# One layer of a hybrid delta-rule and latent-attention encoder: the prompt's latent query projection placed between the two input projections, narrower products in the block inverse, a shared half of PSUM

## Chip, cores and metric

One Trainium2 chip, one core. The metric is device time of one execution in microseconds, the median of several runs.

## What is computed

One encoder layer for two sequences that share weights: a prompt of 1024 tokens (`p`) and a sample of 512 (`s`). All is float32 at the interface.

```
h    = rmsnorm(x);  proj = h @ w_in                    # 2048 -> 5984 columns
qkv  = silu(conv5(qkv))                                # delta-rule heads, 8 of 128
o_a  = gated delta rule forward + backward             # chunks, one inverse per chunk
q    = rmsnorm(c_q) @ w_uq ; kv = rmsnorm(c_kv) @ w_ukv
o_b  = dense softmax attention over all positions      # 8 heads, rope on 64 columns
y    = concat(o_a*silu(z_a), o_b*silu(z_b)) @ w_out
out  = x + rmsnorm(y)
```

## The kernel before

A dense product is three TensorE products: operands are split into a rounded `hi` (float32r) and a rest `lo`, and hi·hi, lo·hi and hi·lo are summed in one PSUM bank (`piece`, L199 to L208, loads a weight piece of 128x512 on SP's queue; `split`, L192 to L197, makes `whi` on ACT and `wlo` on POOL; `ktile`, L218 to L229, issues the products `mm` of L224, L225 and L228). The small products of the delta rule are plain float32, which the profile records as two passes each.

The stages, in order of the program (`run`, from L1221):

1. **Input projection of the prompt** (`in_proj("p", ...)`). For each 128 columns of `w_in` (a strip, 47 of them) 16 k-tiles are summed into two banks. The first two strips run while x arrives, normalised later by `rbh`, which `bcast_cols` makes out of row sums (`xcols`, L275; `bcp`, L190).
2. **Input projection of the sample** (`in_proj("s", ...)`), one bank to a strip, merged with the **delta rule** (`gdn_streams`). The delta rule runs 12 jobs, 8 of one prompt head and 4 of two sample heads, in three streams: `gdn_front` (the masked decays `bc`, L668 and L669, the products `kk`, and a 31-step elimination on VectorE), `gdn_back` (the block inverse: `Dp`, `Fp`, then three rounds of `Tp` at L791 with 128, 64 and 32 moving columns), and `gdn_scan` (per chunk `pk`, `py`, `pu`, each of which waits for VectorE or ScalarE to take up the product before it).
3. **`mla_prep`** for the latent queries: three blocks of 512 tokens (two of the prompt, one of the sample), 12 strips `pq` each, 12 matmuls to a strip (L558 to L560), merged with the delta rule that is still running.
4. **Attention** of the prompt, then of the sample (`kp`, `vp`, `s`, `pt`, `po`), merged with the rest of the delta rule; once the delta rule has ended, with the first half of the **output projection** (`first()`, L1272).
5. The rest of the output projection alone.

In the merged stages the order of TensorE's instructions is written out by `merge` (L136): every stream yields a time at which it wants to go on, `self.t` counts modelled TensorE time (`cost`, L116: 0.42 ns for a column and pass), and the first stream in the list whose time has come is asked next. A stream of the delta rule yields `self.t + self.lat` or `self.t + self.tlat` after each step, so that other streams fill the wait. TensorE executes this order strictly; the other engines' orders come from the scheduler. Outside `merge` the scheduler orders TensorE too.

PSUM in stages 1 and 2 is one pool for each `in_proj`: 6 banks `mm` and 2 `tk` for the prompt, 3 and 1 for the sample beside 4 of the delta rule. Stage 2's pools are opened when those of stage 1 are closed.

Of the kernel before, what the change touches and what calls it, by code (L numbers as in the profile page):

```python
# [17 lines left out]
P = 128  # L18
# [39 lines left out]
class Kern:  # L58
    def __init__(self, ctx, tc, a):
# [21 lines left out]
        self.cols = {}  # L81
        self.t, self.streams, self.leaving, self.busy = 0.0, None, False, [0.0, 0.0]

    def constants(self):
        nc, c, load = self.nc, self.const, self.load
        self.ident = self.kept.tile([P, P], F32, tag="ident", name="ident")
        nc.sync.dma_start(self.ident, self.a["ident"])
# [10 lines left out]
        self.identb = c.tile([P, P], BF16, tag="identb", name="identb")  # L98
        nc.vector.tensor_copy(self.identb, self.ident)
# [81 lines left out]
    def bcast_cols(self, cols, n, ps, out, scale=1.0, tag="tk"):  # L181

        nc = self.nc
        for c0 in range(0, n, 4):
            m = min(4, n - c0)
            pb = ps.tile([P, BLK], F32, tag=tag, name="bcp", bufs=self.tkb)
# [45 lines left out]
    def in_proj(self, q, T, pools, lo_eng, ns, pace):  # L232
        nc, a = self.nc, self.a
        cp, hps, hp, ev, psmm = pools
        psb = psmm
# [7 lines left out]
        newps = lambda: [psmm.tile([P, BLK], F32, tag="mm", name=f"mm{b}") for b in range(nb)]  # L243
# [29 lines left out]
        cols = psb.tile([P, nt], F32, tag="tk", name="xcols", bufs=self.tkb)  # L273
# [7 lines left out]
        yield self.t + BC  # L281
        self.bcast_cols(r, nt, psb, rbh, scale=0.5)

        later = []
        for f in order:
# [9 lines left out]
            if f < 32 or ZB0 <= f < LAST:  # L295
# [20 lines left out]
                if f < 8:  # L316
                    later.append(self.sums(q, f, T, t, acc, cp, ev, psmm))
                if 8 <= f < 24:
                    later.append(self.to_tokens(q, f, T, t, acc, cp, psmm))
            else:  # L320
# [5 lines left out]
                if f < ZB0:  # L326
# [5 lines left out]
                    if f in (CKV0 - 1, ZB0 - 1):  # L332
                        later.append(self.csums(q, f, T, sq, psmm))
                if f == LAST:
                    later.append(self.gates(q, T, acc, ev, psb))

    def sums(self, q, f, T, t, sq, ev, xp, psmm):
# [8 lines left out]
        for b in range(T // BLK):  # L346
            ps = psmm.tile([P, BLK], F32, tag="tk", name="sumps", bufs=self.tkb)
# [14 lines left out]
        ps = psmm.tile([P, H * C], F32, tag="tk", name="qcols", bufs=self.tkb)  # L362
# [23 lines left out]
    def csums(self, q, f, T, sq, psmm):  # L386
# [3 lines left out]
        ps = psmm.tile([P, C], F32, tag="tk", name="csumps", bufs=self.tkb)  # L390
# [7 lines left out]
        yield self.t + 9  # L398
        ps = psmm.tile([P, P], F32, tag="tk", name="crow", bufs=self.tkb)
# [5 lines left out]
    def to_tokens(self, q, f, T, t, sq, ev, psmm):  # L405
# [6 lines left out]
        for c0 in range(0, C, 4):  # L412
            ps = psmm.tile([P, 4, P], F32, tag="tk", name="tokps", bufs=self.tkb)
# [17 lines left out]
    def gates(self, q, T, acc, ev, psb):  # L431
# [4 lines left out]
        for c0 in range(0, C, 8):  # L436
            ps = psb.tile([P, 8, 64], F32, tag="tk", name="abps", bufs=self.tkb)
# [28 lines left out]
        pg = psb.tile([P, 2, C, 16], F32, tag="tk", name="gps", bufs=self.tkb)  # L466
# [4 lines left out]
        yield self.t + 3  # L471
# [13 lines left out]
        for c0 in range(0, C, 4):  # L485
            ps = psb.tile([32, BLK], F32, tag="tk", name="gtps", bufs=self.tkb)
# [13 lines left out]
    def mla_prep(self, blocks, rp, hp, pp, qp, psb):  # L500
# [32 lines left out]
        for b, (q, t0) in enumerate(blocks):  # L533
# [18 lines left out]
            for n, f in enumerate((8, 0, 1, 9, 2, 3, 10, 4, 5, 11, 6, 7)):  # L552
# [3 lines left out]
                ps = psb.tile([P, BLK], F32, tag="pm", name="pq", bufs=PMB)  # L556
# [190 lines left out]
    def gdn_back(self, turn, q, T, heads, env, KQ, UA):  # L747
# [3 lines left out]
        for items in (((0, 0), (1, 4)), ((0, 4), (1, 0))):  # L751
# [469 lines left out]
    def run(self, stop=None):  # L1221
        tc, nc = self.tc, self.nc
        self.tkb, self.wb, self.rb = 2, 4, 4
# [6 lines left out]
        def in_pools(es, q, mm):  # L1230
# [8 lines left out]
            return cp, hps, hp, ev, pool(es, "ps" + q, mm, space=PSUM)  # L1239
# [7 lines left out]
        self.tkb, self.wb, self.rb = 1, 3, 2  # L1247
        with ExitStack() as es:
            env = self.gdn_open(gd, right)
            gdn = self.gdn_streams(jobs, env)  # L1250
            self.merge(self.in_proj("s", TS, in_pools(es, "s", 3), nc.gpsimd, 2, 0.6), gdn)
# [141 lines left out]
```

## Time and profile before

| | |
|---|---|
| median of 3 runs | 3361.96 us (3359.56 to 3369.88) |
| the profiled execution's own time | 3363.58 us |
| its span | 3361.7 us |
| mean granted TensorE clock | 0.983 |
| TensorE (PE) busy | 3212.2 us, 96% of the span |
| VectorE, ScalarE, GpSimd busy | 1735.1, 1283.6, 1158.5 us |
| DMA | 381.66 MB, mean 114 GB/s |

The busy time of TensorE is a union of overlapping records (a matmul is listed with 0.39 us where the next starts 0.23 us later), so the price of a matmul is read from the distance of two starts in the timeline. The granted clock is 1 at 2.4 GHz and 0.5 at 1.2 GHz, and a window's clock is a mean of the two.

### The profile page before, as it was taken

Reading aid. Unit: us, or ns where it says so; the run is one execution under the profiler, and the core shown is the slowest. Engines: PE = TensorE matmul, PEld = TensorE weight load, DVE = VectorE, ACT = ScalarE, POOL = GpSimd, SP = SyncE. Lnnn points to the kernel's source line nnn. Section 1 sums busy time; section 2 is a strip of 40 time slices with the busy share of each in tenths; the row PEclk is TensorE's granted clock in tenths of the full one; section 3 lists DMA queues with packets and bytes.
Section 4 is the critical chain, followed back from the end, with each engine's and each line's share of the span. In section 5 each row is a group of like instructions: output and inputs, shape, how many; then the busy total and the mean of one; then the engine's idle time right before and its main releaser. Section 6 shows DMA issues by size and latency. Waiting matters only on the chain.

```text
span 3361.7 us, 46959 instructions
## 1 busy us (share of the span) xinstructions
PE 3212.2 (96%) x16554; PEld 2688.5 (80%) x16554; DVE 1735.1 (52%) x4000; ACT 1283.6 (38%) x2956; POOL 1158.5 (34%) x1026
## 2 busy tenths in 40 slices
PE   8999999999999899999999989899999989999998
PEld 6888888888887688788788777688898878787876
DVE  7234333443412656774775577688787655331212
ACT  4222222222212334444345334365656555432231
POOL 6322222222223532332332334222222444464452
PEclk9999999999999899999999999899999999999999
DMA  4222222222223534334433466522222242564454
GB/s 159 83 73 79 72 78 75 78 72 79 84 75 105 159 100 126 116 107 129 131 111 120 135 211 206 155 82 70 89 76 64 99 135 86 155 186 135 143 168 135
DMA packets 271404, 381.66 MB, mean 114 GB/s; under 512 B 75632, under 2 KB 126824, under 8 KB 269632
## 3 DMA queue, kind: packets, MB, share of 16 engines
q1 hardware_dynamic: 271168, 378.66, 37.0%
q8 instruction: 130, 2.13, 0.3%
q14 instruction: 106, 0.87, 0.1%
HBM read 286.73 MB, written 88.29 MB: 112 GB/s over the span
## 4 chain that ended last, share of the span: by engine, by line
PE 65%; DVE 15%; DMA 10%; issue 3%; ACT 3%; POOL 2%; SPq 1%; POOLq 0%; DVEq 0%; ACTq 0%
PE mm L224 13%; PE mm L228 12%; PE mm L225 12%; DMA wraw<-w_out 3%; PE py L1152 3%; PE py L1151 3%; PE py L1153 3%; DVE tm L737 3%; DVE XT L739 2%; PE Tp L791 2%; POOL wlo L199 2%; PE pt L1074 2%; DMA wraw<-w_in 1%; DVE UA L686 1%; DVE acc L306 1%
## 5 line engine op out<-in xcount | busy, mean ns | idle before, releaser
L199 POOL TENSOR_TENSOR wlo<-wraw,whi 128x512 fp32r<-128x512 f32 x620 | 832.3, 1346 | 1610.4 <-ACT whi L196 1522.3
L224 PE MATMUL mm<-hi,whi 128*128 128x512 f32 x2256 | 910.6, 405 | 16.9 <-ACT whi L196 11.7
L225 PE MATMUL mm<-lo,whi 128*128 128x512 f32 x2256 | 884.7, 393 | 8.1 <-DVE lo L255 8.1
L196 ACT ACTIVATE whi<-wraw 128x512 fp32r<-128x512 f32 x620 | 389.0, 631 | 1181.5 <-PE mm L225 693.4
L228 PE MATMUL mm<-hi,wlo 128*128 128x512 f32 x2256 | 767.5, 394 | 1.6 <-POOL wlo L199 1.5
L224 PEld LDWEIGHTS mm<-hi,whi 128*128 128x128 f32 x2256 | 429.3, 190 | 101.1 <-ACT whi L196 13.7
L228 PEld LDWEIGHTS mm<-hi,wlo 128*128 128x128 f32 x2256 | 427.7, 190 | 97.1 <-POOL wlo L199 5.0
L225 PEld LDWEIGHTS mm<-lo,whi 128*128 128x128 f32 x2256 | 429.4, 190 | 92.7 <-DVE lo L255 10.0
L1151 PE MATMUL py<-whi,mhi 128*128 128x512 f32 x768 | 304.1, 396 | 9.9 <-DVE y L1166 5.6
L1152 PE MATMUL py<-wlo,mhi 128*128 128x512 f32 x768 | 303.8, 396 | 7.5 <-POOL wlo L199 7.4
L1153 PE MATMUL py<-whi,mlo 128*128 128x512 f32 x768 | 302.8, 394 | 0.0
L1035 POOL TENSOR_TENSOR pe<-pe,af 128x512 f32<-128x512 f32 x160 | 166.8, 1060 | 377.8 <-DVE af L1033 203.9
L306 DVE SCALAR_TENSOR_TENSOR acc<-cin,conv_w,acc 128x1024 f32<-128x1024 f32 (+1 forms) x192 | 219.3, 1142 | 40.8 <-ACT acc L304 33.2
L302 DVE TENSOR_TENSOR cin<-mm,rbh 128x512 f32<-128x512 f32 x72 | 47.4, 687 | 311.6 <-PE mm L228 262.6
L1151 PEld LDWEIGHTS py<-whi,mhi 128*128 128x128 f32 x768 | 145.1, 189 | 45.4 <-DVE y L1166 7.5
L1152 PEld LDWEIGHTS py<-wlo,mhi 128*128 128x128 f32 x768 | 145.2, 189 | 44.3 <-POOL wlo L199 12.8
L1153 PEld LDWEIGHTS py<-whi,mlo 128*128 128x128 f32 x768 | 144.8, 189 | 32.3
L310 DVE TENSOR_TENSOR acc<-mm,rbh 128x512 f32<-128x512 f32 x48 | 31.6, 686 | 231.3 <-PE mm L228 231.3
L1166 DVE TENSOR_TENSOR y<-py,g 128x512 f32<-128x512 f32 x36 | 24.7, 690 | 239.1 <-ACT junk L1165 235.7
L1021 ACT ACTIVATE pe<-s,am 128x512 f32<-128x512 f32 x160 | 110.5, 691 | 92.7 <-DVE am L1020 85.6
L737 DVE TENSOR_TENSOR tm<-XT,lam 128x126 f32<-128x126 f32 (+22 forms) x372 | 128.8, 346 | 23.2 <-ACT lam L729 16.1
L199 DVE TENSOR_TENSOR ptl<-pt,pth 128x512 fp32r<-128x512 f32 x160 | 109.9, 687 | 56.9 <-ACT pth L196 55.8
(449 smaller groups left out, 5251.9 us busy)
## 6 DMA issues: line engine op xcount, KB each, us to landing
wraw<-w_in SPq DMA_DIRECT2D x376, 256.0 KB
wraw<-w_out SPq DMA_DIRECT2D x192, 256.0 KB
dd<-dX SPq DMA_DIRECT2D x48, 256.0 KB
wraw<-w_uq SPq DMA_DIRECT2D x36, 256.0 KB
x<-xT_p SPq DMA_DIRECT2D x16, 512.0 KB
xres<-x_p SPq DMA_DIRECT2D x8, 1024.0 KB
y_p<-y SPq DMA_DIRECT2D x32, 256.0 KB
x<-xT_s SPq DMA_DIRECT2D x16, 256.0 KB
```

Source lines behind the costliest of these rows:

```text
L196: nc.scalar.activation(hi, src, AF.Copy)
L199: (lo_eng or nc.vector).tensor_sub(lo, src, hi.bitcast(F32))
L224: nc.tensor.matmul(ps, whi[:, k], hi[:, s], start=kt == 0, stop=False)
L225: nc.tensor.matmul(ps, whi[:, k], lo[:, s], start=False, stop=False)
L228: nc.tensor.matmul(ps, wlo[:, k], hi[:, s], start=False, stop=kt == KT - 1)
L306: nc.vector.scalar_tensor_tensor(acc, cin[:, j:j + T], w[:, f, j:j + 1], acc, op0=ALU.mult, op1=ALU.add)
L737: nc.vector.tensor_mul(tv, XT[:, :m, j:j + 1].to_broadcast([P, m, n]), lam[j // 16][:, j % 16:j % 16 + 1, j + 1:].to_broadcast([P, m, n]))
L1021: nc.scalar.activation(pe[k], o, AF.Exp, bias=m[:, k:k + 1], scale=-1.0, accum_out=l[:, k:k + 1])
L1035: nc.gpsimd.tensor_mul(pe[k2], pe[k2], f[:, k2:k2 + 1].to_broadcast([P, BLK]))
L1151: nc.tensor.matmul(ps, hi[:, c], w[0], start=kt == kts[0], stop=False)
L1152: nc.tensor.matmul(ps, hi[:, c], w[1], start=False, stop=False)
L1153: nc.tensor.matmul(ps, lo[:, c], w[0], start=False, stop=kt == kts[1] - 1)
```

## The change

- `mla_prep` of the prompt's two blocks is called alone, between the two input projections; the later call has the sample's block only. The sample's `in_proj` pools are opened before it.
- PSUM: two pools, `psA` and `psB`, of 3 `mm` banks and 1 `tk` bank each. A strip of the prompt takes one bank of each. `psA` stays for the sample; `psB` serves `mla_prep`'s products and is then closed for the delta rule. `tk` banks are dealt out in turn (`self.tk`).
- `in_proj` runs a third strip before `bcast_cols`; three waits in `csums` and `gates` are longer by 5.
- `Tp` multiplies only the columns of `F` whose rows are used: 64 in the second round, 32 in the third, into the matching rows of PSUM.
- The identity of the mask product and the masks are float32r in place of bfloat16.

```diff
-        self.ident = self.kept.tile([P, P], F32, tag="ident", name="ident")
-        nc.sync.dma_start(self.ident, self.a["ident"])
+        self.identb = self.kept.tile([P, P], F32R, tag="ident", name="ident")
+        raw = self.sm.tile([P, P], F32, tag="diag", name="iraw")
+        nc.sync.dma_start(raw, self.a["ident"])
+        nc.vector.tensor_copy(self.identb, raw)
+        self.ident = self.identb.bitcast(F32)
...
-            m = c.tile([P, P], BF16, tag=f"mask{i}", name=f"mask{i}")
+            m = c.tile([P, P], F32R, tag=f"mask{i}", name=f"mask{i}")
...
+    def tk(self, shape, name):
+
+        self.tkn += 1
+        return self.tks[self.tkn % len(self.tks)].tile(shape, F32, tag="tk", name=name, bufs=1)
...
-        newps = lambda: [psmm.tile([P, BLK], F32, tag="mm", name=f"mm{b}") for b in range(nb)]
+        newps = lambda: [psmm[b].tile([P, BLK], F32, tag="mm", name=f"mm{b}", bufs=3) for b in range(nb)]
...
-        yield self.t + BC
-        self.bcast_cols(r, nt, psb, rbh, scale=0.5)
+
+        heads.append(newps())
+        yield from self.strip(a["w_in"][order[ns]], ops, heads[-1], lo_eng)
+        self.bcast_cols(r, nt, rbh, scale=0.5)
...
-        yield self.t + 9
-        ps = psmm.tile([P, P], F32, tag="tk", name="crow", bufs=self.tkb)
+        yield self.t + 14
+        ps = self.tk([P, P], "crow")
...
-                        nc.tensor.matmul(ps[:, i], F[:, i], cur[:, i, cs], start=True, stop=True)
+                        nc.tensor.matmul(ps[ms, i], F[:, i, ms], cur[:, i, cs], start=True, stop=True)
...
+        ea, eb, ex = ExitStack(), ExitStack(), ExitStack()
+        banks = [pool(ea, "psA", space=PSUM), pool(eb, "psB", space=PSUM)]
+        self.tks = list(banks)
         with ExitStack() as es:
-            self.spawn(self.in_proj("p", TP, in_pools(es, "p", 6), nc.gpsimd, 2, 2.7))
+            self.spawn(self.in_proj("p", TP, in_pools(es, "p", banks), nc.gpsimd, 2, 2.7))
...
+        spools = in_pools(ex, "s", banks)
+        wps = self.wp
+        with ExitStack() as es:
+            self.spawn(self.mla_prep([("p", 0), ("p", BLK)], *prep_pools(es), banks[1], "mm", 3))
+        eb.close()
+        self.tks.pop()
...
-                prep = [pool(e1, "prep" + n) for n in "rhwx"] + [pool(e1, "psP", space=PSUM)]
-                self.merge(self.mla_prep([("p", 0), ("p", BLK), ("s", 0)], *prep), gdn)
+                self.merge(self.mla_prep([("s", 0)], *prep_pools(e1), pool(e1, "psP", space=PSUM)), gdn)
```

How TensorE's order moves, at three places. `mm` is an input projection, `hi6` and `hi7` the sample's k-tiles 6 and 7, `bc` the first decay of the delta rule, `pq` a latent query strip.

At the switch from prompt to sample, before: the delta rule's first product follows the sample's k-tile 6.

```order
L224 MATMUL mm0_7590<-hi6_7681,whi_7655 128x512
L225 MATMUL mm0_7590<-lo6_7682,whi_7655 128x512
L228 MATMUL mm0_7590<-hi6_7681,wlo_7656 128x512
L668 MATMUL bc_7695<-ghlp_659,ident_r_556 128x512
L669 LDWEIGHTS identb_550
L669 MATMUL bc_7695<-mask0_552,identb_550 128x512
```

In the changed kernel, at the end of the 288 `pq` matmuls, which follow k-tile 6 there with nothing between them:

```order
L566 MATMUL pq_8249<-chi_7940,whi_8245 128x512
L567 MATMUL pq_8249<-clo_7941,whi_8245 128x512
L568 MATMUL pq_8249<-chi_7940,wlo_8246 128x512
L676 MATMUL bc_8416<-ghlp_784,ident_r_559 128x512
L677 MATMUL bc_8416<-mask0_555,ident_533 128x512
L676 MATMUL bc_8424<-ghlp_784,ident_r_559 128x512
L677 MATMUL bc_8424<-mask1_557,ident_533 128x512
L231 MATMUL mm0_8310<-hi7_8435,whi_8370 128x512
```

The delta rule and the sample's k-tiles 7 to 15 now stand behind the prompt's whole latent query projection.

In the inverse, before: the third round of `Tp`, between the sample's `mm` and the scan's `pk`.

```order
L224 MATMUL mm_9016<-hi_7866,whi 128x512
L225 MATMUL mm_9016<-lo_7867,whi 128x512
L228 MATMUL mm_9016<-hi_7866,wlo 128x512
L791 MATMUL Tp<-UA,F 128x32 x8
L832 MATMUL pk<-st,KQ 128x128 x2
L835 MATMUL pk<-st,KQ 128x128 x2
```

And in the changed kernel at the like place:

```order
L231 MATMUL mm_9910<-hi_8435,whi 128x512
L232 MATMUL mm_9910<-lo_8436,whi 128x512
L235 MATMUL mm_9910<-hi_8435,wlo 128x512
L799 MATMUL Tp<-UA,F 32x32 x8
L840 MATMUL pk<-st,KQ 128x128 x2
L843 MATMUL pk<-st,KQ 128x128 x2
```

The place is the same, with 32 columns of `F` in place of 128.

At the last scan steps of the delta rule, before: attention (`s`, `pt`, `po`) stands between `pu` and `pk`, as at every later step.

```order
L1053 MATMUL po<-pth,vl 128x256
L1013 MATMUL s<-kh,qh 128x512
L1014 MATMUL s<-kl,qh 128x512
L1015 MATMUL s<-kh,ql 128x512
L1016 MATMUL s<-krs,qr 128x512
L1017 MATMUL s<-krl,qr 128x512
L832 MATMUL pk<-st,KQ 128x128 x4
L835 MATMUL pk<-st,KQ 128x128 x4
L1074 MATMUL pt<-ident,pe 128x128 x4
```

In the changed kernel the last steps stand next to each other, up to the sample's first `kp`:

```order
L862 MATMUL py<-r,UA 128x128 x4
L878 MATMUL pu<-yk,ktok 128x128 x4
L881 MATMUL pu<-yb,UA 128x128 x4
L840 MATMUL pk<-st,KQ 128x128 x4
L843 MATMUL pk<-st,KQ 128x128 x4
L972 MATMUL kp<-ch,whi 128x512
L973 MATMUL kp<-cl,whi 128x512
L974 MATMUL kp<-ch,wlo 128x512
```

The prompt's attention has run out there before the delta rule; six changes from one scan product to the next have nothing between them, and none had before.

## Rows read from the trace of the kernel before

**Rows 1.** The page: busy time of the engines, and the granted clock in 40 slices.
```profile
PE 3212.2 (96%) x16554; PEld 2688.5 (80%) x16554; DVE 1735.1 (52%) x4000; ACT 1283.6 (38%) x2956; POOL 1158.5 (34%) x1026
...
PEclk9999999999999899999999999899999999999999
```

**Rows 2.** Windows by stage: us, then busy (instructions) PE, PEld, DVE, ACT, POOL; clock, DMA share, GB/s.
```profile
0.00:70.00 70.00, 54.28 (x214) 42.73 (x215) 59.51 (x52) 33.04 (x38) 48.00 (x37) 0.95 0.52 175
70.00:1070.00 1000.00, 1000.00 (x4509) 828.75 (x4509) 336.37 (x481) 243.92 (x381) 267.92 (x243) 1.00 0.24 75
1070.00:1250.00 180.00, 161.18 (x726) 129.35 (x725) 107.08 (x259) 70.13 (x142) 86.74 (x78) 0.91 0.48 150
1250.00:1945.00 695.00, 670.49 (x3768) 567.14 (x3767) 443.24 (x1214) 299.61 (x795) 214.53 (x217) 0.99 0.41 121
1945.00:2200.00 255.00, 224.27 (x1245) 189.23 (x1244) 184.80 (x452) 99.80 (x270) 87.63 (x70) 0.93 0.61 186
2200.00:2580.00 380.00, 366.03 (x2576) 329.42 (x2576) 312.32 (x971) 231.10 (x685) 103.94 (x104) 1.00 0.25 73
2580.00:2880.00 300.00, 281.87 (x1597) 238.87 (x1596) 172.62 (x364) 159.37 (x361) 123.78 (x109) 0.98 0.35 106
2880.00:3361.00 481.00, 454.11 (x1932) 363.01 (x1930) 119.12 (x212) 146.62 (x286) 225.97 (x170) 0.98 0.52 158
```

**Rows 3.** PE waits, 1070 to 1245 us: us, times, longest.
```profile
PE bcp L190 <- DVE diag L189: 4.9, 1, 4.9
```

**Rows 4.** Window of 20 us at the switch, columns as in rows 2.
```profile
1080.00:1100.00 20.00, 15.05 (x54) 11.30 (x55) 14.60 (x13) 8.76 (x19) 15.89 (x12) 0.83 0.83 277
```

**Rows 5.** SP timeline at the switch: start, us, engine, line, what.
```profile
1086.85 0.66 SPq L315 DMA_DIRECT2D f45p<-ct  x1
```

**Rows 6.** PE timeline in the prep stage: first and last of eight pq matmuls in a row.
```profile
1989.03 0.39 PE L559 MATMUL pq<-clo,whi 128*128 128x512 f32 x1
...
1990.65 0.39 PE L560 MATMUL pq<-chi,wlo 128*128 128x512 f32 x1
```

**Rows 7.** Group by form: weight loads of L791: count, busy, mean ns, idle before.
```profile
L791 PEld LDWEIGHTS Tp<-UA,F 128*128 128x128 f32 x768 | 91.7, 192 | 4.1 <-DVE z L919 1.1 <-ACT dec L673 0.4 <-DVE UA L793 0.2
```

**Rows 8.** PE timeline in the attention stage: second and third round of Tp.
```profile
2378.60 1.89 PE L791 MATMUL Tp<-UA,F 128*128 128x64 f32 x16
2380.33 0.61 PE L1074 MATMUL pt<-ident,pe 128*128 128x128 f32 x4
...
2382.88 1.87 PE L791 MATMUL Tp<-UA,F 128*128 128x32 f32 x16
2384.58 0.63 PE L1074 MATMUL pt<-ident,pe 128*128 128x128 f32 x4
```

**Rows 9.** PE timeline around a product whose weights are 8 columns wide.
```profile
169.45 0.39 PE L225 MATMUL mm<-lo,whi 128*128 128x512 f32 x1
169.68 0.27 PE L400 MATMUL crow<-ident,cy 128*8 128x128 f32 x1
...
170.26 0.62 PE L228 MATMUL mm<-hi,wlo 128*128 128x512 f32 x2
```

**Rows 10.** PE timeline around products that use 64 rows of the array.
```profile
97.29 0.39 PE L225 MATMUL mm<-lo,whi 128*128 128x512 f32 x1
97.61 0.46 PE L439 MATMUL abps<-ident,cacc 64*128 64x64 f32 x4
...
98.56 0.40 PE L228 MATMUL mm<-hi,wlo 128*128 128x512 f32 x1
```

**Rows 11.** PE timeline of a scan step that hardly waited.
```profile
1246.93 0.61 PE L873 MATMUL pu<-yb,UA 128*128 128x128 f32 x4
1247.38 1.06 PE L791 MATMUL Tp<-dd,F 128*128 128x128 f32 x8
...
1249.41 0.71 PE L832 MATMUL pk<-st,KQ 128*128 128x128 f32 x4
```

**Rows 12.** PE timeline of a scan step that waited, in the prep stage.
```profile
2019.54 0.61 PE L873 MATMUL pu<-yb,UA 128*128 128x128 f32 x4
...
2024.61 0.80 PE L832 MATMUL pk<-st,KQ 128*128 128x128 f32 x2 [3.76 <-DVE oacc L888]
```

More of the change, by code (lines that the diff above doesn't have):

```diff
@@ L81, in __init__ @@
         self.cols = {}
+        self.tks, self.tkn = [], 0
         self.t, self.streams, self.leaving, self.busy = 0.0, None, False, [0.0, 0.0]
@@ L179, in rsqrt, with bcast_cols @@
         return y
-    def bcast_cols(self, cols, n, ps, out, scale=1.0, tag="tk"):
+    def bcast_cols(self, cols, n, out, scale=1.0):
         nc = self.nc
@@ L185, in bcast_cols @@
             m = min(4, n - c0)
-            pb = ps.tile([P, BLK], F32, tag=tag, name="bcp", bufs=self.tkb)
+            pb = self.tk([P, BLK], "bcp")
             for c in range(m):
@@ L272, in in_proj @@
         yield self.t + 2
-        cols = psb.tile([P, nt], F32, tag="tk", name="xcols", bufs=self.tkb)
+        cols = self.tk([P, nt], "xcols")
         for c in range(nt):
@@ L316, in in_proj @@
                 if f < 8:
-                    later.append(self.sums(q, f, T, t, acc, cp, ev, psmm))
+                    later.append(self.sums(q, f, T, t, acc, cp))
                 if 8 <= f < 24:
-                    later.append(self.to_tokens(q, f, T, t, acc, cp, psmm))
+                    later.append(self.to_tokens(q, f, T, t, acc, cp))
             else:
@@ L332, in in_proj, with sums @@
                     if f in (CKV0 - 1, ZB0 - 1):
-                        later.append(self.csums(q, f, T, sq, psmm))
+                        later.append(self.csums(q, f, T, sq))
                 if f == LAST:
-                    later.append(self.gates(q, T, acc, ev, psb))
-    def sums(self, q, f, T, t, sq, ev, xp, psmm):
+                    later.append(self.gates(q, T, acc, ev))
+    def sums(self, q, f, T, t, sq, ev):
         nc, C = self.nc, T // P
@@ L346, in sums @@
         for b in range(T // BLK):
-            ps = psmm.tile([P, BLK], F32, tag="tk", name="sumps", bufs=self.tkb)
+            ps = self.tk([P, BLK], "sumps")
             bs = slice(b * BLK, (b + 1) * BLK)
@@ L361, in sums @@
         yield self.t + 4
-        ps = psmm.tile([P, H * C], F32, tag="tk", name="qcols", bufs=self.tkb)
+        ps = self.tk([P, H * C], "qcols")
         nc.tensor.transpose(ps, r, self.ident[:H * C, :H * C])
@@ L384, in knorms, with csums @@
             self.cols["cc", d, h, q], self.cols["kd", d, h, q] = cc, kd
-    def csums(self, q, f, T, sq, psmm):
+    def csums(self, q, f, T, sq):
         nc, C = self.nc, T // P
         yield self.t + 6
-        ps = psmm.tile([P, C], F32, tag="tk", name="csumps", bufs=self.tkb)
+        ps = self.tk([P, C], "csumps")
         for c in range(C):
@@ L403, in csums, with to_tokens @@
         nc.sync.dma_start(self.dt("r" + name + q, [1, T]).rearrange("a (c p) -> (a c) p", c=C), row[:C])
[L405 removed]
+    def to_tokens(self, q, f, T, t, sq, ev):
         nc, C = self.nc, T // P
@@ L412, in to_tokens @@
         for c0 in range(0, C, 4):
-            ps = psmm.tile([P, 4, P], F32, tag="tk", name="tokps", bufs=self.tkb)
+            ps = self.tk([P, 4, P], "tokps")
             for i in range(4):
@@ L429, in to_tokens, with gates @@
             self.knorms(q, f - 8, C, sk)
-    def gates(self, q, T, acc, ev, psb):
+    def gates(self, q, T, acc, ev):
         nc, sm, c = self.nc, self.sm, self.const
@@ L436, in gates @@
         for c0 in range(0, C, 8):
-            ps = psb.tile([P, 8, 64], F32, tag="tk", name="abps", bufs=self.tkb)
+            ps = self.tk([P, 8, 64], "abps")
             for i in range(min(8, C - c0)):
@@ L465, in gates @@
         nc.vector.tensor_mul(lw, lw, self.nea.unsqueeze(1).to_broadcast([P, C, 16]))
-        pg = psb.tile([P, 2, C, 16], F32, tag="tk", name="gps", bufs=self.tkb)
+        pg = self.tk([P, 2, C, 16], "gps")
         ps, ps2 = pg[:, 0], pg[:, 1]
@@ L470, in gates @@
         nc.tensor.matmul(ps2, self.ones, lw, start=True, stop=True)
-        yield self.t + 3
+        yield self.t + 8
         gc = tl("gc")
@@ L485, in gates @@
         for c0 in range(0, C, 4):
-            ps = psb.tile([32, BLK], F32, tag="tk", name="gtps", bufs=self.tkb)
+            ps = self.tk([P, BLK], "gtps")[:32]
             for i in range(4):
@@ L497, in gates, with mla_prep @@
         self.g[q] = dict(beta=beta, ngc=ngc, nege=nege, ege=e, kdf=kdf, egl=egl, ghl=ghl)
-    def mla_prep(self, blocks, rp, hp, pp, qp, psb):
+    def mla_prep(self, blocks, rp, hp, pp, qp, psb, tag="pm", banks=PMB):
         nc, a, S = self.nc, self.a, self.scratch
@@ L555, in mla_prep @@
                     raws = load(*blocks[b + 1])
-                ps = psb.tile([P, BLK], F32, tag="pm", name="pq", bufs=PMB)
+                ps = psb.tile([P, BLK], F32, tag=tag, name="pq", bufs=banks)
                 for k in range(4):
@@ L1222, in run @@
         tc, nc = self.tc, self.nc
-        self.tkb, self.wb, self.rb = 2, 4, 4
+        self.wb, self.rb = 4, 4
         TP, TS = 1024, 512
@@ L1229, in run, with in_pools @@
         left, right = "left", "right"
-        def in_pools(es, q, mm):
+        def in_pools(es, q, banks):
             cp = pool(es, "cin" + q, 2)
```

18 lines of the change are left out of this document (9 added, 9 removed).

## The prediction

> **What bounds the kernel.** The page first: TensorE is busy 96% of the span at a granted clock near 1 almost throughout [rows 1], and no other engine is over 52%. So the kernel is TensorE's work plus what TensorE loses, and the second view is the table of windows by stage [rows 2]. In it the loss of a stage is the idle time (its length less PE's busy time) plus the time given away by the clock (its length times one minus the clock). The prompt's projection, 70 to 1070 us, loses nothing. The switch to the sample, 1070 to 1250, loses 18.8 + 16.2 = 35 us. The sample's projection with the delta rule, 1250 to 1945, loses 24.5 + 7 = 31.5. The latent query stage with the start of attention, 1945 to 2200, loses 30.7 + 17.9 = 48.6, the worst rate of all. Attention with the delta rule, 2200 to 2580, loses 14 in 380 us, although DVE is 82% busy there. Attention with the output projection, to 2880, loses 18.1 + 6 = 24, and the rest 36. A change can gain by less work on TensorE, or by moving work from a stage that loses much to one that loses little.
>
> The sum below is made against the profiled execution's own 3363.6 us, which is 1.6 us above the median of the runs; I call a change real beyond 0.3%, or 10 us.
>
> **Narrower Tp: less work.** In the timeline 16 passes with 64 moving columns take 2380.33 − 2378.60 = 1.73 us, and 16 with 32 moving columns 2384.58 − 2382.88 = 1.70 us [rows 8]: 0.107 us a pass, whatever moves. The weight loads, 128 columns for each pass, are what is alike in both [rows 7]. There are 768 passes, 24 groups of 16 in each round. If the load's share goes with its columns, the second round falls to half (saves 0.87 us a group, 20.8 in all) and the third to a quarter (1.28 a group, 30.6 in all), 51.4 at most. At worst nothing is saved, if a load or an issue has a floor at 0.107. The narrowest weights in the trace are 8 columns: from 169.45 to 170.26 stand two `mm`, one such product with 128 moving columns and the start of the next `mm` pair [rows 9]. An `mm` or `pq` step is 0.231 us (seven steps from 1989.03 to 1990.65 [rows 6]), and this stretch holds three of them, so 0.81 − 0.69 = 0.12 is left for the narrow product: its own moving time and nearly nothing for entering and leaving. I take 20.8 for the second round and, since no row shows a step as short as 0.027, three quarters of 30.6 for the third: **−44**.
>
> Not all of it arrives. Counted in the timeline of before, 16 of the 48 groups stand between two products of the scan, and in 13 of those there is at most 1.4 us of other work. A scan product starts 2.03 us behind the last work of its forerunner at the earliest (1247.38 to 1249.41, filled there by `Tp` alone [rows 11]) and waits for VectorE or ScalarE if the filling is shorter. With 0.9 us taken out of a filling that was just enough, the wait comes back: 13 × 0.9 = **+12**. The other 32 groups stand beside `mm` or attention work that does not wait for them.
>
> **The prompt's latent queries at the switch.** The 288 `pq` matmuls cost 288 × 0.231 = 66.5 us in both places, so only the losses count. At the switch they stand behind the sample's k-tile 6. Until then nothing changes: TensorE waits for x, with 15.05 us busy of 20 at a clock of 0.83 while DMA moves 277 GB/s [rows 4]. The first piece of `w_uq` stands on SP's queue behind the store of strip 45, which was issued at 1086.85 [rows 5], and behind 33 loads of 0.26 MB counted from k-tile 6's x on; at 277 GB/s these 8.7 MB, begun near 1072, are through at 1103. So the first `pq` starts near 1105, about where the delta rule's first product started before, and this part of the loss, some 22 us, stays. Behind it 66 us of dense work lets the sample's remaining x, `hi` and `lo` land. The 4.9 us wait of `bcp` goes [rows 3], since a third strip stands before it. Of the 13 us lost after 1105 I keep 5: **−8**.
>
> **The latent query stage.** One block in place of three. Its start (the loads of `c_q`, the first split) and the start of attention keep their losses, about 18 us each; the 13 us in the middle fall to a third: **−9**. The delta rule that ran beside the two blocks now runs beside attention, some 100 us more at that stage's rate of 14 in 380: **+4**.
>
> **The end of the delta rule.** This is what is late next. The delta rule starts 67 us later against attention, the prompt's attention ends first, and `first()` may not start the output projection before the delta rule is over. The order shows six changes from one scan product to the next with nothing between, and two with under 1.1 us. None was unfilled before, so the price is bounded: 2.0 us at least [rows 11], and 4.7 at most, from the last of four `pu` that start at 2019.54 to `pk` at 2024.61 [rows 12]. I take 2.7, near the lower end, because the larger one was taken in the stage with the most transfers, 186 GB/s [rows 2]: 6 × 2.7 + 2 = **+18**. The clock may fall in that stretch; at the lowest price it does not. The output projection that no longer runs beside attention runs alone instead, at 36 us lost in 481 against 24 in 300, which is no difference.
>
> **The rest at nothing.** The float32r mask moves the same 512 columns behind the same `mm`; the third strip and the new identity copy lie in the prompt's start, where 70 to 1070 is full [rows 2]; the `tk` banks stay two for the prompt and one for the sample; the longer waits in `csums` and `gates` are filled by `mm`. If `mm` were short there, each would cost a scan-like 2 us.
>
> Sum: −44 + 12 − 8 − 9 + 4 + 18 = −27, so 3337 in the profiled execution and **3335** as a median.
>
> **A rule that speaks against the narrow Tp.** The eight-column row shows an entering and leaving of about 0.01 us [rows 9]; products on half the rows of the array cost more: from 97.29 to 98.56 there are three `mm` (0.69) and four products of 64 columns (0.21 at 0.107 for 128), so 0.37 us is left for entering and leaving [rows 10]. The Trainium skill, TensorEngine Tiling, section Key Properties, says that changing the tiling mode drains TensorE. The trace agrees for row tiles and not for the one column tile. Another of its pages, TensorE: Matmul & The Clock Gate, section Back-to-back issue gap, gives steps of 60 cycles for up to 64 columns, which would make the third round's saving whole and the sum 3327 (an estimate by that page).
>
> **Rivals.**
> - *Every narrow round drains.* 48 excursions at the 0.37 us of rows 10 cost 18 us: 3353. For it: mode 128x64 is in no row. Against it: rows 9. Chance 0.15.
> - *The switch is bound by transfers.* If the loads of the latent queries, on top of the sample's x, hold `pq` back all through (0.5 MB in and out for each 2.8 us strip is 190 GB/s, beside 16 loads), the 66 us take 90: 3359. Against it: 277 GB/s was reached [rows 4]. Chance 0.12.
> - *The recurrence binds* (the slow side). If the delta rule advances by its own latency and not by TensorE's time, it ends 67 us later, and that time stands unfilled in place of the 18 + 4: 3335 + 67 − 22 = 3380. It decides from 57 us unfilled on, over 20 changes at 2.7 in place of six. Against it: the order has six, and between 2200 and 2580 TensorE is 96% busy. Chance 0.07.
> - *All of it arrives.* Tp gives 51 with little given back and the unfilled steps cost 2.0: 3335 − 7 − 8 − 6 = 3314, less if the middle of the switch loses nothing. Chance 0.13.
>
> **Numbers.** The forecast has 0.53. Its own range is 3312 to 3352 by the bounds of Tp and of the scan step. Faster than 3352: the forecast and the last rival nearly whole, 0.63, half of the drain and a third of the transfers, 0.12: 0.75. Within 10 us: the other parts of these, 0.16. Slower: the recurrence and the tail of the transfers, 0.09. The range takes in the drain and the transfers: 3295 to 3362.
>
> **What would show it.** Right: Tp groups of 16 passes in 0.9 and 0.4 to 0.6 us; `pq` steps of 0.23 without gaps from about 1105 to 1175; no wait at `bcp`; windows from there to the sample's strips with PE near full; six waits of 2 to 3 us at the last `pk`, `py`, `pu`, with the prompt's last `po` ahead of them. Wrong: a start of `mm` 0.3 us late behind each Tp group; a first `pq` after 1115; more than ten waits of the scan; Tp groups still at 1.7 us.

## Result and profile after

| | before | after |
|---|---|---|
| median | 3360.76 us (3355.85 to 3369.88, 4 runs) | 3409.86 us (3406.47 to 3415.35, 4 runs) |
| span of the profiled execution | 3361.7 us | 3413.4 us |
| TensorE busy | 3212.2 us, 96% | 3190.3 us, 93% |
| mean granted clock | 0.983 | 0.978 |

The ratio is 1.0144, 95% interval 1.0118 to 1.0171: slower by 49 us, where the prediction had 3335 us and a range up to 3362.

The page of after, to be read against [rows 1]: less work on TensorE, in a longer span, and a clock dip near the end of the delta rule (slice 32 of 40, 2645 to 2731 us).

```profile
PE 3190.3 (93%) x16554; PEld 2651.4 (78%) x16554; DVE 1749.2 (51%) x4000; ACT 1283.5 (38%) x2956; POOL 1161.5 (34%) x1026
...
PEclk9999999999999999999999999999999899999999
```

**The narrow products do what they should.** The timeline of after at two `Tp` groups, against [rows 8], and the groups of their weight loads, against [rows 7]:

```profile
2410.58 0.97 PE L799 MATMUL Tp<-UA,F 128*64 128x64 f32 x16
2411.47 0.66 PE L1082 MATMUL pt<-ident,pe 128*128 128x128 f32 x4
...
2413.92 0.59 PE L799 MATMUL Tp<-UA,F 128*32 128x32 f32 x16
2414.44 0.39 PE L1059 MATMUL po<-pth,vh 128*128 128x256 f32 x1
```

```profile
L799 PEld LDWEIGHTS Tp<-UA,F 128*64 128x64 f32 x384 | 20.1, 137 | 9.6 <-ACT dec L681 4.3 <-issue 1.4 <-ACT whi L203 0.7
L799 PEld LDWEIGHTS Tp<-UA,F 128*32 128x32 f32 x384 | 12.1, 113 | 8.7 <-issue 2.5 <-DVE tm L745 1.4 <-DVE UA L694 1.1
```

A group of 16 passes takes 2411.47 − 2410.58 = 0.89 us in place of 1.73, and 2414.44 − 2413.92 = 0.52 in place of 1.70. Half of 1.73 would be 0.87 and a quarter of 1.70 would be 0.43, so at most 0.1 us a group is left for entering and leaving. With 24 groups in each round that is 24 × (0.84 + 1.18) = 48 us less for TensorE.

**The losses eat it twice over.** Windows by stage of after, columns as in [rows 2]: the switch up to the first `Dp`, the sample's projection, the sample's latent queries, attention with the delta rule up to the first output product, attention with the output projection, the rest.

```profile
1070.00:1297.00 227.00, 185.74 (x752) 144.86 (x751) 126.34 (x219) 68.75 (x122) 121.92 (x95) 0.91 0.60 194
1297.00:2030.00 733.00, 694.04 (x3989) 580.53 (x3988) 476.90 (x1291) 318.69 (x842) 232.46 (x235) 0.99 0.41 122
2030.00:2116.00 86.00, 61.15 (x334) 48.20 (x332) 62.16 (x138) 24.93 (x61) 26.37 (x21) 0.91 0.48 144
2116.00:2786.00 670.00, 599.51 (x4096) 525.44 (x4097) 510.69 (x1504) 381.59 (x1092) 176.66 (x176) 0.96 0.29 85
2786.00:2881.00 95.00, 90.30 (x508) 74.90 (x507) 55.59 (x105) 50.34 (x111) 36.88 (x32) 1.00 0.37 107
2881.00:3413.00 532.00, 507.35 (x2177) 408.75 (x2175) 119.65 (x213) 163.12 (x314) 252.00 (x190) 0.99 0.50 153
```

The like windows of the kernel before with nothing but the narrow `Tp` (the first experiment below), which is the measure for the rest of the change:

```profile
1070.00:1188.00 118.00, 99.33 (x406) 77.78 (x405) 68.42 (x149) 44.36 (x84) 64.25 (x56) 0.91 0.56 175
1188.00:1922.00 734.00, 704.23 (x4085) 585.44 (x4084) 479.20 (x1323) 323.20 (x853) 237.33 (x239) 0.99 0.42 123
1922.00:2138.00 216.00, 185.17 (x1043) 151.73 (x1041) 159.85 (x383) 82.84 (x229) 76.21 (x60) 0.94 0.65 202
2138.00:2588.00 450.00, 419.99 (x2969) 367.88 (x2968) 366.90 (x1099) 271.62 (x781) 125.76 (x126) 0.99 0.28 85
2588.00:2846.00 258.00, 245.98 (x1394) 208.87 (x1393) 146.92 (x303) 136.07 (x305) 109.31 (x96) 0.99 0.33 96
2846.00:3324.00 478.00, 454.83 (x1945) 365.80 (x1944) 118.21 (x213) 146.83 (x287) 226.52 (x171) 0.99 0.52 159
```

Idle time is length less PE's busy time. It rises by 41.3 − 18.7 = 23 us at the switch, by 39.0 − 29.8 = 9 in the sample's projection, and by 70.5 − 30.0 = 40 beside attention, where the clock also falls from 0.99 to 0.96; the latent query stage gives back 30.8 − 24.9 = 6.

**At the switch** the new products wait for their weights. The waits of PE from 1070 to 1195 us, the waits of ACT from 1090, and PE's timeline:

```profile
PE pq L566 <- ACT whi L203: 11.9, 1, 11.9
...
PE pq L567 <- DVE clo L549: 3.3, 1, 3.3
PE pq L566 <- DVE rx L572: 3.2, 2, 1.9
```

```profile
ACT whi L203 <- DMA wraw<-w_uq: 31.6, 11, 6.6
```

```profile
1098.22 0.40 PE L235 MATMUL mm<-hi,wlo 128*128 128x512 f32 x1
1110.55 0.79 PE L566 MATMUL pq<-chi,whi 128*128 128x512 f32 x1 [11.93 <-ACT whi L203]
```

The first `pq` starts at 1110.55, behind 11.93 us in which TensorE has nothing else. ACT stands 31.6 us for pieces of `w_uq` in this stretch, but TensorE's own waits behind the first `pq` are short: 3.3 and 3.2 us for VectorE.

### The profile page after: what moved, and what is told of

It is laid out like the page before. It is cut to its first block, busy times and chain, and to the rows that moved or that the text cites. A ratio compares the mean times of both kernels' runs of the same rounds, so it can differ in the third digit from the quotient of the medians.

```text
span 3413.4 us, 47006 instructions
## 1 busy us (share of the span) xinstructions
PE 3190.3 (93%) x16554; PEld 2651.4 (78%) x16554; DVE 1749.2 (51%) x4000; ACT 1283.5 (38%) x2956; POOL 1161.5 (34%) x1026
## 5 line engine op out<-in xcount | busy, mean ns | idle before, releaser
L318 DVE TENSOR_TENSOR acc<-mm,rbh 128x512 f32<-128x512 f32 x48 | 31.6, 686 | 235.8 <-PE mm L235 235.8
L1082 PE MATMUL pt<-ident,pe 128*128 128x128 f32 x640 | 102.6, 281 | 42.3 <-DVE ptl L206 16.7
```

The lines of the kernel that those rows point to most:

```text
L1082: nc.tensor.transpose(pt[:, j, i * P:(i + 1) * P], b["pes"][i][k][:, c:c + P], self.ident)
```

## Experiments

All are timed against the kernel before on the same chip. "Narrow" is the kernel before with the narrow `Tp`; it is what a part is added to. "The planner" is `merge` with its modelled times, and "output products" are those of the output projection.

### The four parts apart

**e1_tp_only**: the kernel before with the change's line of `Tp` alone.

```diff
-                        nc.tensor.matmul(ps[:, i], F[:, i], cur[:, i, cs], start=True, stop=True)
+                        nc.tensor.matmul(ps[ms, i], F[:, i, ms], cur[:, i, cs], start=True, stop=True)
```

> The kernel before with the narrow Tp alone (64 and 32 columns of F). Theory A, the early latent query projection costs the time and the narrow Tp gives what its rows show: 52 us less work, some 15 to 25 us of it returned as waits, so 3361 - 32 = 3329 us, between 3320 and 3340. Theory B, narrow tiles upset TensorE (drains, waits of the scan) and the early projection is harmless: 3361 us or slower.

Measured 3329.63 us, ratio 0.9898 (0.9881 to 0.9916). **e2_wide_tp** is the reverse: the changed kernel with that line taken back.

> The changed kernel with Tp back at 128 columns. Theory A: it loses the 52 us of work and gets some waits back, 3410 + 25 = 3435 us, between 3425 and 3450. Theory B: it is as fast as or faster than the changed kernel, 3410 us or less.

Measured 3437.88, ratio 1.0215 (1.0197 to 1.0234). The narrow product gives 35 us on the kernel before and 28 on the changed one; theory B falls.

**e3_late_prep**: the changed kernel with the prompt's latent queries moved back beside the delta rule.

```diff
-            self.spawn(self.mla_prep([("p", 0), ("p", BLK)], *prep_pools(es), banks[1], "mm", 3))
...
-                self.merge(self.mla_prep([("s", 0)], ...), gdn)
+                self.merge(self.mla_prep([("p", 0), ("p", BLK), ("s", 0)], ...), gdn)
```

> The changed kernel with the prompt's latent query projection back behind the sample's input projection, beside the delta rule; PSUM halves, third strip, longer waits, masks and narrow Tp stay. Theory A: within 8 us of the run with the narrow Tp alone, about 3325 us, since the third strip also saves the 5 us wait of bcp. A third theory C, that the PSUM halves or the third strip cost: 3350 us or more.

Measured 3393.43, ratio 1.0082 (1.0067 to 1.0098). A miss for theory A: with the part that I held for the costly one gone, 64 us over narrow are still there. **e4_no_delay**: the changed kernel with `DELAY = 0.0` in place of 25, the planned wait between the two attentions.

> The changed kernel without the pause between the prompt's and the sample's attention (25 us of the model's time). Theory A, in which 30 us are lost where the last scan steps stand alone: the sample's attention fills part of them, 5 to 15 us faster, 3395 to 3405 us. If the pause does not matter there, or the sample's attention takes the loss along: 3410 us within 4.

Measured 3396.77, ratio 1.0097 (1.0079 to 1.0115), 13 us off; what that means shows in e18 below.

### What the 64 us are

**e5_third_strip** adds to narrow the third strip alone, **e6_long_waits** the longer waits (two lines; the one in `csums` is passed for two norms, so three waits in each projection), **e7b_f32r_mask** the float32r masks and identity (edits as in the change). **e8_psum_only** is e3 with these three taken back, so it keeps the PSUM halves and the narrow `Tp`.

```diff
-        yield self.t + BC
+        heads.append(newps())
+        yield from self.strip(a["w_in"][order[ns]], ops, heads[-1], lo_eng)
```

> Before with the narrow tiles, and the third strip ahead of the row sums' broadcast (no fixed wait there) for both projections, nothing else. H1 (the third strip carries the 64 us by which the kernel with late latent projections, 3393, stands behind the narrow tiles alone, 3330): 3380 to 3400, and the first delta rule's Dp comes some 20 us later than at 1188 us. H2, H3, H4 (the longer waits, the f32r mask, the PSUM halves): within 10 us of 3330. H5 (no part alone; the shifted modelled times order the later stages anew): 3335 to 3365, with the loss mostly behind 2137 us, beside the attention.

> Before with the narrow tiles and the two longer waits (14 for 9 ahead of the latent norm's row, 8 for 3 in the gates). H2: 3380 to 3400. H1, H3, H4: within 10 us of 3330. H5: 3335 to 3365.

> Before with the narrow tiles, and the masks and the unit matrix in f32r as in the change. By rows it costs nothing: the mask matmul takes 403 ns in the kernel with late latent projections against 395 ns with bf16, x48 0.4 us. H3: 3380 to 3400. All others: 3325 to 3335.

> The kernel with late latent projections, with the third strip, the longer waits and the f32r mask taken back too: what is left of the change is the PSUM halves, the shared turn of the tk tiles, the order in which the pools open, and the narrow tiles. H4: 3380 to 3400. H1, H2, H3: 3325 to 3340. H5: 3335 to 3365.

Measured, in this order: 3385.51 (1.0074, 1.005 to 1.0097), 3338.31 (0.9929, 0.9911 to 0.9948), 3330.09 (0.9907, 0.9886 to 0.9929), 3333.49 (0.9915, 0.9893 to 0.9937). Over narrow that is 56 + 9 + 0 + 4 = 69, near the 64; the 0 and the 4 lie within the intervals. Nearly all of it is the third strip. **e9_third_prompt** and **e10_third_sample** have it for one sequence each (`if q == "p":` and `if q == "s":`, else the old wait).

> Narrow tiles, and the third strip ahead of the broadcast for the prompt alone. Third strip in both projections: 3386; in neither: 3330. If the sample's strip carries the loss (theory O, below, or P): 3325 to 3335. If the prompt's does: 3375 to 3390.

> Narrow tiles, and the third strip for the sample alone. Theory O (the strip takes the place of a wait in the planner's modelled time, so that the planner hands out another order of delta rule and projection from there to the end) and theory P (three finished strips stand in the three mm banks until the broadcast, and their evictions come in a bunch on VectorE) both 3375 to 3390; the prompt's strip as the cause: 3325 to 3340.

Measured 3334.64 (0.9908, 0.989 to 0.9926) and 3383.82 (1.0051, 1.0033 to 1.007): the sample's strip, of 48 products, carries 54 us. The products are the same in number, only earlier. Is it their place or the order that `merge` makes behind them? **e11_old_plan** has the strip early for both, but tells the planner the old story:

```diff
+        heads.append(newps())
+        t1 = self.t
+        for _ in self.strip(a["w_in"][order[ns]], ops, heads[-1], lo_eng):
+            self.t = t1
         yield self.t + BC
...
             if heads:
+                if f == order[ns]:
+                    for _ in range(KT):
+                        self.cost(BLK * nb, 3)
+                        yield self.t
                 pss = heads.pop(0)
```

> Narrow tiles, the third strip ahead of the broadcast in both projections, but the sample's costs the planner nothing there, the fixed wait of 8 follows it, and the strip's modelled time is spent where the strip stood before: all other TensorE instructions keep the order of the kernel with narrow tiles alone. Theory O: 3325 to 3345. Theory P: 3375 to 3390.

Measured 3332.02, ratio 0.9892 (0.9876 to 0.9907): the loss is gone, with the strip still there. The reverse test, **e13_bc0**, has no strip and one constant changed, `BC = 0` for 8; **e15_bc12** has `BC = 12`.

> Narrow tiles alone, and the planner's fixed wait ahead of the broadcast 0 in place of 8: no third strip, no other instruction. Its order of TensorE is, at every mark that was counted (delta rule products done by the last projection product, by the first key product of the attention; output products done by the last product with the values: 294 in place of 361), that of the kernel with the sample's third strip. Theory O (the order handed out): 3375 to 3395, the late marks as with the sample's third strip (attention's first key product 2150, delta rule's last product near 2607). If the strip itself carries the loss: 3330 to 3340 (up to 8 us of wait for the row sums' root).

> Narrow tiles alone, the fixed wait 12 in place of 8 (367 output products ahead of the attention's last product in place of 361). Theory O: 3318 to 3332. Otherwise 3330 to 3336.

Measured 3381.61 (1.0047, 1.0032 to 1.0062) and 3350.43 (0.9955, 0.9938 to 0.9972). e13 is theory O's number: without a strip, and with a planned wait of 0 in place of 8, 52 us are lost where the sample's strip lost 54. TensorE waits 4.9 us for `bcp` in e13, as it does in narrow, so the loss is not there. The traces show the orders whole. Of TensorE's 16554 products, in order of their starts and by the names of their tiles, e10 and e13 agree in all but 88 places, which lie between 4889 and 5069, about the moved strip; narrow and e11 agree in all but 234, all before 4949; but narrow and e10 differ in 8624 places, from 4889 to 14610. Each of the two pairs with one order agrees within 3 us (3384 and 3382, 3330 and 3332), though only one kernel of each has the early strip. e15 is a miss: by the count of output products it should have been the best, and it is 21 us slower than narrow. The order makes the time; that count does not rank orders.

Where an order loses is seen in e13's windows (sample's projection, attention with the delta rule) and its group of `pt`, beside narrow's windows above and narrow's group below:

```profile
1200.00:1934.00 734.00, 693.34 (x3990) 573.88 (x3989) 474.36 (x1289) 318.73 (x841) 234.69 (x236) 0.99 0.41 122
...
2157.00:2672.00 515.00, 470.09 (x3294) 409.53 (x3295) 412.95 (x1226) 309.42 (x879) 143.45 (x142) 0.99 0.28 86
```

```profile
L1074 PE MATMUL pt<-ident,pe 128*128 128x128 f32 x640 | 100.6, 278 | 40.3 <-DVE ptl L199 21.2 <-POOL pe L1035 8.4 <-DVE amm L1029 7.6
```

In narrow the same group, with two more that are needed further down:

```profile
L1074 PE MATMUL pt<-ident,pe 128*128 128x128 f32 x640 | 100.0, 278 | 22.7 <-DVE ptl L199 15.0 <-DVE amm L1029 3.2 <-POOL pe L1035 2.2
...
L964 PE MATMUL kp<-ch,whi 128*128 128x512 f32 x48 | 20.2, 421 | 0.0
...
L917 PE MATMUL oT<-ident,oacc 128*128 128x128 f32 x96 | 14.7, 276 | 1.9 <-ACT dec L673 1.9
```

Idle time is 41 for 30 us in the sample's projection and 45 for 30 beside attention. Attention's transposes wait 40.3 us for VectorE and GpSimd in place of 22.7: the same instructions, dealt so that they come before their operands are made.

### The early latent queries

**e12_early_prep**: the changed kernel without the third strip and the longer waits.

```diff
-        heads.append(newps())
-        yield from self.strip(a["w_in"][order[ns]], ops, heads[-1], lo_eng)
+        yield self.t + BC
...
-        yield self.t + 14
+        yield self.t + 9
...
-        yield self.t + 8
+        yield self.t + 3
```

> The changed kernel without the third strip and the longer waits: the prompt's latent projections early, the PSUM halves, the narrow tiles and the f32r masks stay. If the parts add (early projections +16, PSUM halves +3 over 3330): 3340 to 3355. If the early projections cost only together with the strip: 3310 to 3330, as the prediction's sum had it. If they cost more by themselves (no slack in the modelled order to lose): 3360 to 3390.

Measured 3374.39, ratio 1.0034 (1.0021 to 1.0048): 41 us over e8, which differs from it by the early queries (and the mask, priced at 0 by e7b). They are not additive with the strip: 41 here, 16 between e3 and after. Its windows, as above, the switch also in three parts (up to the first `pq`, the `pq`, behind them) and the attention stage in two:

```profile
1070.00:1283.00 213.00, 174.85 (x701) 137.56 (x700) 121.28 (x205) 65.95 (x117) 116.01 (x91) 0.90 0.63 201
...
1070.00:1109.00 39.00, 22.72 (x86) 17.51 (x85) 30.22 (x27) 18.44 (x29) 26.36 (x20) 0.80 0.84 273
1109.00:1190.00 81.00, 72.62 (x288) 56.75 (x287) 46.48 (x52) 19.10 (x31) 52.80 (x39) 0.93 0.63 206
1190.00:1283.00 93.00, 79.52 (x328) 63.30 (x329) 44.58 (x128) 28.41 (x58) 36.86 (x34) 0.91 0.54 166
...
2021.00:2103.00 82.00, 62.25 (x349) 51.69 (x347) 58.32 (x147) 28.51 (x79) 24.80 (x21) 0.88 0.56 166
2103.00:2719.00 616.00, 560.56 (x3896) 491.63 (x3897) 484.50 (x1443) 361.53 (x1037) 169.45 (x167) 0.97 0.29 86
...
2103.00:2610.00 507.00, 471.59 (x3306) 414.33 (x3307) 411.19 (x1254) 300.32 (x864) 134.81 (x136) 0.98 0.27 80
2610.00:2719.00 109.00, 88.97 (x592) 77.30 (x591) 73.31 (x190) 61.21 (x173) 34.64 (x31) 0.94 0.37 114
```

Narrow's attention stage in the like two parts:

```profile
2138.00:2479.00 341.00, 317.25 (x2268) 277.18 (x2267) 287.37 (x874) 203.96 (x590) 92.67 (x95) 0.99 0.28 83
2479.00:2588.00 109.00, 102.74 (x703) 90.70 (x702) 79.53 (x226) 67.66 (x191) 33.09 (x31) 0.97 0.28 90
```

With the clock's share (length times one minus the clock) added to the idle time, the switch loses 38 + 21 = 59 us against 19 + 11 = 29 in narrow, the latent stage 20 + 10 = 30 against 31 + 13 = 44, and attention with the delta rule 55 + 18 = 74 against 30 + 4 = 34. The switch's 59 are 24 up to the first `pq`, 14 within the `pq` and 22 behind them. The attention's 40 more are 18 in the longer first part (46 against 27) and 17 in the last 109 us, where the delta rule runs out (27 against 10); the rest is rounding of the clock. **e17_late_delta** leaves the queries late and gives attention as much of the delta rule, by a later start:

```diff
+            for st in gdn:
+                st[1] = self.t + 100
             self.merge(self.in_proj("s", TS, in_pools(es, "s", 3), nc.gpsimd, 2, 0.6), gdn)
```

> Narrow tiles alone, all latent projections late as before, but the planner lets the delta rule start 100 us of modelled time after the sample's projection. It then enters the attention as far back as with the early projections (376 of 640 pk products done against 384; 448 without the hold), and 166 output products stand ahead of the attention's last product in both. Theory D (the early projections cost by what they leave of the delta rule for the attention): the stage of attention and delta rule loses 60 to 70 us as there (37 without the hold), 20 to 24 in the gap behind it, and the time is 3355 to 3385. Theory W (they cost by standing alone, waiting for weights and at a low clock): 3330 to 3345.

Measured 3376.58, ratio 1.0044 (1.0029 to 1.0058). The stage of attention and delta rule, in e17:

```profile
2102.00:2721.00 619.00, 561.35 (x3924) 491.17 (x3925) 488.80 (x1455) 364.38 (x1048) 168.50 (x167) 0.97 0.29 86
```

It is 619 us long with 58 idle, against 616 and 55 in e12. Its waits are those of e12 too. Three groups of e17, then of e12:

```profile
L1074 PE MATMUL pt<-ident,pe 128*128 128x128 f32 x640 | 100.8, 279 | 35.2 <-DVE ptl L199 19.3 <-POOL pe L1035 6.4 <-DVE al L1031 3.5
...
L964 PE MATMUL kp<-ch,whi 128*128 128x512 f32 x48 | 20.7, 431 | 11.9 <-DMA qp<-qr0p 11.9
...
L917 PE MATMUL oT<-ident,oacc 128*128 128x128 f32 x96 | 15.8, 290 | 7.3 <-ACT oacc L903 7.3
```

```profile
L1080 PE MATMUL pt<-ident,pe 128*128 128x128 f32 x640 | 100.3, 278 | 32.1 <-DVE ptl L206 23.1 <-POOL pe L1041 5.5 <-DVE al L1037 1.5
...
L970 PE MATMUL kp<-ch,whi 128*128 128x512 f32 x48 | 21.7, 452 | 9.3 <-DMA qp<-qr0p 8.1 <-ACT pe L1027 1.2
...
L923 PE MATMUL oT<-ident,oacc 128*128 128x128 f32 x96 | 15.8, 290 | 7.4 <-ACT oacc L909 7.3 <-ACT dec L679 0.2
```

So theory D holds for attention's 40 us: with as much of the delta rule left over for it, attention loses as much, wherever the queries ran. That the whole times agree too is partly luck, for the kernels lose the rest at different places. e12 loses 30 us more than narrow at the switch, of which the latent stage gives back 14 and attention with the output projection 7 (8 lost in place of 15). e17 loses 45 + 20 = 65 us in its latent stage, against 44 in narrow:

```profile
1878.00:2102.00 224.00, 178.96 (x952) 145.00 (x950) 157.38 (x365) 74.24 (x197) 78.19 (x60) 0.91 0.62 189
```

**e14_after_wait12** and **e16_after_wait20** put a planned wait of 12 and of 20 between strip and broadcast of the changed kernel (`yield self.t + 12`, `yield self.t + 20`).

> The changed kernel with a planned wait of 12 between the third strip and the broadcast, nothing else. Output products ahead of the attention's last product: 283 in place of 133. Theory O: 3335 to 3365 (the early projections then keep the 12 to 26 us that stand in rows at the switch). If the early projections and the strip cost by what they are and not by the order that follows: 3400 to 3420, with the wait on top.

> The changed kernel with a planned wait of 20 there (178 output products ahead of the attention's last product: a longer wait and a worse order than with 12). Theory O: 3365 to 3395, some 25 to 40 us over the wait of 12. A cost or gain that goes with the length of the wait: within 10 us of the wait of 12, on either side.

Measured 3388.12 (1.0069, 1.0052 to 1.0087) and 3360.29 (0.9985, 0.9975 to 0.9995). Both numbers missed, in opposite directions, and yet they say that theory O is right in kind: the changed kernel gets 22 and 50 us faster by a number that does no work, and the longer wait is the better one. Their windows of attention with the delta rule, e14 first:

```profile
2153.00:2702.00 549.00, 501.92 (x3462) 441.13 (x3463) 434.30 (x1301) 324.56 (x926) 150.58 (x150) 0.96 0.27 82
...
2105.00:2704.00 599.00, 548.18 (x3823) 481.56 (x3824) 472.43 (x1430) 352.09 (x1021) 162.84 (x162) 0.97 0.28 84
```

Set beside the others, this stage's loss rises with what is left of the delta rule when attention begins, counted in the traces as the `pk` products that start before the first `kp`:

| `pk` done, of 640 | kernel | stage, us | lost, idle + clock, us | whole, us |
|---|---|---|---|---|
| 448 | narrow | 450 | 30 + 4 = 34 | 3330 |
| 448 | e15 | 436 | 30 + 4 = 34 | 3350 |
| 440 | e13 | 515 | 45 + 5 = 50 | 3382 |
| 416 | e14 | 549 | 47 + 22 = 69 | 3388 |
| 384 | e16 | 599 | 51 + 18 = 69 | 3360 |
| 384 | e12 | 616 | 55 + 18 = 74 | 3374 |
| 376 | e17 | 619 | 58 + 19 = 76 | 3377 |
| 360 | e4 | 670 | 64 + 13 = 77 | 3397 |
| 360 | after | 670 | 70 + 27 = 97 | 3410 |

That speaks for theory D beyond e17, though these orders differ in more than this count. It does not rank whole times: e15 has narrow's loss in this stage and is 21 us slower, and of the five kernels in the middle e16, with 384 done, is the fastest and e14, with 416, the slowest.

**e18_tp_no_delay**: narrow with `DELAY = 0.0`.

> Narrow tiles alone, and no planned delay between the prompt's attention and the sample's. On the changed kernel the same took 13 us off. If that is the delay's own: 3315 to 3325. If it came of the order that the changed kernel happened to have: 3325 to 3350.

Measured 3341.10, ratio 0.9942 (0.9925 to 0.9958): 11 us slower than narrow, where the same edit took 13 off the changed kernel. Its gain in e4 was that order's.

## Why the prediction was wrong

The prediction's sum was −27 us; measured, with each experiment against its neighbour, it is −35 (e1) + 4 (e8) + 41 (e12) + 36 (after over e12) = +46, near the 49 of the result.

- **Narrower Tp, −44 + 12: right in size.** −35 measured for −32. The groups save 48: from before to e1 TensorE's busy time falls by 48.2 us (3212.2 to 3164.0), but the span by 37.0, so 11 come back as idle time. The mechanism of the +12 is borne out for a third of that: the scan's products `pk`, `py` and `pu`, on which it was counted, wait 37.5 us in place of 33.8; `kk` takes 3.0 more and `pt` 2.4. The third round takes 0.52 us, within the 0.4 to 0.6 foretold. The rival *Every narrow round drains* is out. The Trainium skill, TensorEngine Tiling, section Key Properties, says that changing the tiling mode drains TensorE; at column tiles of 64 and 32 this trace shows no such gap. The bound on it is the 0.1 us a group above, where the rival needed 0.37.
- **"The rest at nothing": failed.** The third strip was put at nothing because 70 to 1070 us is full in the prompt. In the prompt it does cost nothing (e9, 5 us). The step failed for the sample, where the strip replaced a wait that `merge` counts, and so changed the order of all that follows: 54 us on narrow (e10), and together with the longer waits, not taken apart there, 36 on top of the early queries. The mask (e7b) and the PSUM halves (e8) were rightly put at or near nothing; the longer waits cost 9 by e6.
- **"Of the 13 us lost after 1105 I keep 5: −8": failed.** The switch loses 30 us more in e12's window and not 8 less. The part ahead of the first `pq`, which was to keep some 22, was about right: 24 in e12. What was wrong is what follows. The `pq` were taken as dense; in after they run from 1110.55 to 1189.5, 79 us for 66.5, with 14 us lost among them in e12 to waits for VectorE and to the clock. And the stretch behind them, in which the 13 us were to shrink to 5, loses 22 in e12, where TensorE waits 11.9 us at small products of the sample's broadcast and gates (`bcp`, `abps`, `gps`, `gtps`) and 2.5 at `bc`, at a clock of 0.91. The wait of `bcp` is 2.8 us in after, not gone. The rival *The switch is bound by transfers* (66 us take 90) had the place and half of the size: 13 us within the `pq` in place of its 24.
- **The latent query stage, −9: right in kind**, −14 by e12's windows.
- **Delta rule beside attention, "at that stage's rate of 14 in 380: +4": failed.** The rate was read from the stretch of before in which attention and the rest of the delta rule fitted. In e12, where 166 us more of that stage run, its first part loses 18 us more than in narrow.
- **The end of the delta rule, 6 × 2.7 + 2 = +18: right in size without the strip, too small with it.** In e12 the last 109 us lose 17 more than in narrow. In after they lose 28 us idle and 14 by the clock, 42 against narrow's 10, so +32:

```profile
2677.00:2786.00 109.00, 81.27 (x455) 68.43 (x451) 62.13 (x148) 51.45 (x145) 28.22 (x25) 0.87 0.37 114
```

The scan's waits, which were to make the price, are these:

```profile
PE pu L878 <- ACT yb L871: 4.8, 3, 2.9
PE pk L840 <- DVE oacc L896: 3.5, 3, 2.4
...
PE py L862 <- DVE oacc L852: 1.7, 1, 1.7
PE py L862 <- ACT oacc L855: 1.5, 1, 1.5
```

Eight waits, 11.5 us, longest 2.9; the prediction had six of 2 to 3 us. The other 16 us of idle time stand at other products, 7.8 of them at `pt` for VectorE. The clock, which the prediction expected not to fall at its lowest price, was 0.87 there and cost 14 us that no term held. The rival *The recurrence binds* would have needed 57 us of scan waits; over the whole of after they come to 38, as in narrow. The slow side came about, but not by its mechanism.

The terms for the early queries were −8 − 9 + 4 + 18 = +5 in the prediction, and e12 stands 41 over e8: most of the miss is the switch, then the stage beside attention. What stays open is which feature of an order sets its whole time. The kernels with the narrow `Tp`, early or late queries and one wait or another lie between 3330 and 3410 us; the count of output products ahead of the attention's last product, on which e13 to e16 were sized, was right for e13 and wrong for the three others. No order was sought that suits the early queries; the best of the five with them (e16) stands 31 us behind narrow. The kernel before with the narrow `Tp` alone (e1, 3329.63 us) beats both before and after; e7b and e11, within 3 us of it, are no different by their intervals, and no kernel was clearly faster.

## What to carry to other kernels

Where an order is computed from modelled times, no edit that adds, removes or replaces a modelled wait can be taken as free: compare the whole order row by row, and price such an edit by a run of the old order with the new work, as e11 did. Judge a part of a change only together with one or two neighbouring values of its waits, since 50 us lay in one constant here. And before work is moved away from a stage, ask what the filler that it was for the slower chain is replaced by: here the delta rule fell back into attention, and lost there 40 us that no row at the new place shows.

## What was not expected of the hardware

A float32 pass goes with the columns of its weights all the way down: 1.73 / 16 = 108 ns with 128, 0.89 / 16 = 56 ns with 64, and 0.52 / 16 = 33 ns with 32, at 64 and 32 moving columns. Each round's moving columns are the same before and after, so it is the weights that make the difference. Products with full weights follow with at most 0.1 us lost a group. Against it stand the 0.37 us that entering and leaving cost for products on half of the rows [rows 10].
